# Layer 1's experts with 32 slots each, two experts on the tensor engine at once

## The chip, the core and the metric

The kernel is one program on one core of a Trainium2 chip. A core has a tensor engine (PE; its weight loads are listed apart, as PEld), a vector engine (DVE), a scalar engine (ACT), GpSimd (POOL), and SyncE (SP), which in this kernel issues every DMA. The metric is the device time of one run in microseconds (us), as the median of the runs; less is better.

## The reference, cut to what matters

The model has two layers (0 and 1). A layer mixes the tokens (attention, RWKV-7, mLSTM) and then sends them through a mixture of 32 SwiGLU experts. Layer 0 works on 512 tokens; layer 1, the last, on 256. The router picks one of four groups of eight experts for a token, and two experts of that group:

```python
def expert_block(args):
    xb, e = args                                  # rows of the tokens that chose expert e
    gate, up = jnp.split(xb @ w_gu[e], 2, axis=-1)     # w_gu[e]: 1024 x 1024
    return (jax.nn.silu(gate) * up) @ w_down[e]        # w_down[e]: 512 x 1024
...
out = jnp.zeros((N, D), f32).at[st].add(ys[dest] * sw[:, None])
```

All numbers are float32. The weights of one expert are 12 slices of 128 x 1024 (eight of `w_gu`, four of `w_down`), 0.524 MB each. On the reference's own inputs the router gives the 32 experts of layer 0 between 19 and 50 tokens each, and those of layer 1 between 6 and 24.

## The kernel before, in words

Each layer has a mixing phase and an expert phase (`moe_phase`). The order in which instructions stand on each engine is the order in which the program emits them; every engine works through its own list in order, and semaphores hold it where an operand or a buffer is not ready.

The expert phase goes through the experts one by one, with a fixed number of 64 slots for the tokens of each. For each expert `e` these stages are emitted, spread over the loop's steps so that neighbours mix:

- `stageA` (every second expert): picks the rows of two experts' tokens by products with a 0/1 matrix (`select`, `gather`) and transposes them (`turn`) into `xs`.
- `stageB(e, k)` for k from 0 to 7: products of `xs` (128 x 64) with slice k of the gate and up weights. The gate half of the columns goes to rows 0 to 63 of the PSUM bank, the up half to rows 64 to 127: two groups of 64 columns of the array. A float32 product shows as two records in the trace, so a slice is four records. After k = 7 ACT copies the bank to `rows`.
- `rows_of(e)`: one product with `rkT`, from which DVE makes the scatter matrix `selt`. There is one per expert.
- `swiglu`: four transposes on PE, silu on ACT, a product on DVE, giving `at`.
- `stageD(e, f)` for f from 0 to 3: products of `at` with the slices of `w_down`, again in two groups of 64 columns; then `parts`: for each half n of the columns ACT writes weighted rows of one half of the bank (`yy`) and DVE what rounding left, to the other half.
- `stageS`: four products that scatter `yy` to the tokens, in layer 1 added up over all experts in four PSUM banks (`acc`).

The weights come by the function `feeder`. It has a list of slices in the order of use (`seq`: for each expert four gate/up slices, the four down slices of the expert before, four more gate/up slices) and, in layer 1, buffers for 29 slices: one of four, ten of two, five of one. `pump` puts the next slices of the list into the next free buffer and emits a DMA for each run of slices that are neighbours in memory; `done(e, k)` counts a buffer's slices down where the program has emitted their last use, and calls `pump` again. On the chip the DMA waits on SP until PE has done that last use. DMAs take turns on eight landing semaphores, and an issue waits for the landing of the eighth before it.

Before the second expert the program emits `rest()`: what the routing still owes (ranks turned, slot weights `wsl`, and a flag `need` that tells whether any expert has more tokens than slots). After the last expert that flag is read, and only if it is set does a loop over blocks of 64 further slots run, with the weights loaded again for each block.

Ahead of layer 0's mixing, and partly within it, stands the conditioning: products of a small stationary tile with the slices `adaw`, in four groups of 32 columns.

Behind the experts of layer 1 lie the last sums on DVE, the final norm and the store of the output.

Of the kernel before, what the change touches and what calls it, by code (L numbers as in the profile page):

```python
# [20 lines left out]
SLOTS = 64  # L21
# [8 lines left out]
# columns of w_in by block: (first column, width); the gates' block carries repeats as filler  # L30
# [44 lines left out]
# columns of the per-layer parameter tile  # L75
# [8 lines left out]
# columns of the constants  # L84
CC = {}
_o = 0
for _n, _w in (("id", 128), ("perm", 128), ("cos", 256), ("sin", 256), ("mND", 256), ("mI", 128),
               ("bd", 64), ("neg", 256), ("blk", 128), ("tri", 128), ("ones", 128),
               ("rst64", 512), ("rst128", 512), ("hsel", 2), ("ie", 32), ("iot4", 4),
               ("s64", 128), ("sm", 64), ("pm", 1)):  # L90
    CC[_n] = (_o, _o + _w)
    _o += _w
# [3 lines left out]
# which stream's step comes next in the mixing of each layer  # L96
# [21 lines left out]
class Streams:  # L118
    """streams of instructions, merged step by step in the order of emission.

    A stream yields what its next step needs: None, a flag or a tuple of flags.
    """
# [13 lines left out]
    def step(self, it):  # L136
        """the stream's next step; True when it was the last"""
# [5 lines left out]
    def run(self, streams):  # L143
        """in the given order (a character per step, the first stream is "A"), or in turns"""
# [19 lines left out]
def program(tc, I, out, dbg=None, stop=None):  # L164
# [67 lines left out]
    # ---------------- dram scratch  # L232
# [30 lines left out]
    # ---------------- conditioning  # L263
# [26 lines left out]
    def mix_phase(l, last, TT0, hp, hr, rp, rt):  # L290
        X0 = 256 if last else 0           # first token of blocks that only feed outputs
        S0 = TT0 // 2                     # first segment with outputs
# [11 lines left out]
        def L(name, shape=(128, 512)):  # L304
            """outlasts the tiles of H"""
# [5 lines left out]
        def rsq(o, x, scale, eps, n):  # L311
            """o = (x * scale + eps) ** -0.5 on few columns"""
# [10 lines left out]
        # ================= conditioning: 1024 columns at a time, a quarter on each quarter of the rows  # L323
        def ada(la, pairs, first=None):
            """two groups at a time, on each quarter of the rows half a group"""
# [15 lines left out]
            for gi, g in enumerate(pairs):  # L341
# [15 lines left out]
                # columns of the shifts and scales, rows of the rest  # L357
# [12 lines left out]
        def consts():  # L370
            """the parameters and the other constants, behind what comes first"""
# [8 lines left out]
        # ================= norm, transpose  # L380
        hT = {}

        def norm():
# [39 lines left out]
            for k in range(KT):  # L423
# [4 lines left out]
                onact = k in (0, 2, 3, 5, 6)                # a bank is read by one engine  # L428
# [18 lines left out]
        # ================= input projection: weights loaded ahead, split one block ahead  # L447
# [56 lines left out]
        def by_tokens(name, o):  # L504
            """a block of the projection with the tokens on the rows"""
# [10 lines left out]
        # ================= differential attention  # L516
# [3 lines left out]
        def lam():  # L520
# [10 lines left out]
            stt(nlam, le[:, 1:2], -lam_init, le[:, 0:1], ADD, SUB)      # -(lam)  # L531
# [5 lines left out]
        def da_head(h):  # L537
# [3 lines left out]
            def rope(name, o, t0):  # L541
                """ctx columns copied, x columns turned"""
# [19 lines left out]
            # rounded parts and what is left on the two halves of the rows  # L562
# [69 lines left out]
        # ================= RWKV  # L632
# [60 lines left out]
        def rw_stack():  # L693
            """the operands of the small products, each below the other: rounded, what is left, rounded"""
# [24 lines left out]
        def rw_kk(b):  # L719
            """normalised keys, decays and rates of one pair of heads"""  # L720
# [45 lines left out]
        def rw_elem(d, b):  # L766
# [15 lines left out]
            pin = H("pin")                                  # half of the inverse decay  # L782
# [16 lines left out]
            km = H("km")                                    # twice the key  # L799
# [30 lines left out]
        def rw_scores(d, b):  # L830
# [3 lines left out]
            md_all = MDt[0]                                   # [row in its block, column, unit]  # L834
            ae, kp, bt = AB[d, b]
            LT[d, b] = H1("LT", [128, 4, 2, 32])              # the other 32-block of a chunk
            for j in range(4):
# [12 lines left out]
                nd = H1("nq", [128, 2, 2, 64])                # k or b, head  # L850
# [47 lines left out]
        def rw_chunks(d, b):  # L898
            """the inverses of the 64-blocks from those of their 32-blocks; turned, for products"""
# [8 lines left out]
            ks = [slice(64 * c + 32 * d, 64 * c + 32 * d + 32) for c in range(2)]       # sources  # L908
            os = [slice(64 * c + 32 - 32 * d, 64 * c + 64 - 32 * d) for c in range(2)]  # targets
# [19 lines left out]
        def rw_chain(d, b):  # L929
            """solves and the state's recursion for one direction and pair of heads"""  # L930
# [19 lines left out]
            for step in range(4):  # L950
# [18 lines left out]
                if full:  # L969
                    qr = H1("qr", [128, 2, 2, 64])            # [source in the chunk, k or b, head, target]  # L970
# [7 lines left out]
                # two chunks: G, B; yc  # L978
# [69 lines left out]
        def ln64(Y, eps, name, T2):  # L1048
            """layer norm over 64 columns of a [128, 512] tile in place; two token tiles"""
# [43 lines left out]
        # ================= mLSTM  # L1093
        ml = {"mk": {}, "mq": {}, "so": {}}

        def ml_post():
# [5 lines left out]
            for n in [x for x in order if x[0] == "m"]:  # L1102
# [17 lines left out]
                else:                                 # twice silu of the convolution  # L1120
# [582 lines left out]
    def moe_phase(l, last, TT0, rp, mp, rt):  # L1703
# [74 lines left out]
        def stageB(e, k):  # L1778
            if k == 0:
                GU[e] = PS()  # L1780
# [30 lines left out]
        def stageD(e, f):  # L1811
            if f == 0:
                PY[e] = PS()
# [267 lines left out]
```

## Time and profile before

| what | value |
|---|---|
| median of 3 runs | 1975.69 us (1973.17, 1975.69, 1977.97) |
| span of the profiled execution, first to last instruction | 1967.8 us |
| PE busy over the span | 1814.8 us (92%) |
| DVE, ACT, POOL busy | 1045.8, 614.2, 586.9 us |
| moved by DMA | 540.72 MB, mean 275 GB/s |
| expert phase of layer 1, first to last issue of its weights | 1417 to 1917 us |

The page of the profile gives the span of the profiled execution and no other time of it; the median of the runs is 7.9 us above that span. Busy times of PE come from modelled ends of matmuls, so that a busy PE says that products were in flight, and not that it was at its best. A DMA share of 1 means that the sixteen DMA engines of the core had packets in hand all the time.

### The profile page before, as it was taken

To read this page: it belongs to the slowest core of one execution; us is meant where nothing else is said; L and a number is where in the kernel's file an instruction comes from. 1 tells how busy PE (TensorE), PEld (TensorE's weight loads), DVE (VectorE), ACT (ScalarE), POOL (GpSimd) and SP (SyncE) were. 2 spreads that over 40 slices of the span, in tenths; PEclk is the share of its full clock that TensorE was granted. 3 is DMA by queue.
4 is the path that set the end of the run, shared out by engine and by line. 5 is a ranking of instruction groups with operands and counts; after the bars stand their busy time and mean duration, and the time that the engine had idled before them with its cause. 6 is when DMAs were issued, how large, how long until landed. Compare 5 with 4: busy or idle time off the path is not lost. (4 is left out here: it accounts for less than half of the span.)

```text
span 1967.8 us, 29955 instructions
## 1 busy us (share of the span) xinstructions
PE 1814.8 (92%) x11356; PEld 958.3 (49%) x11357; DVE 1045.8 (53%) x2156; ACT 614.2 (31%) x1308; POOL 586.9 (30%) x479
## 2 busy tenths in 40 slices
PE   6999999989699999999999598899869999999996
PEld 2666776656343333333333376767633333333332
DVE  3798656657545555455455689876752222221223
ACT  2453546641111111111111355447512112111121
POOL 1440222314135555655566453222310000000000
PEclk9999999988799999999999799989989999999998
DMA  8465646563979999999995333312589999999992
GB/s 337 138 219 183 201 142 220 209 216 125 368 294 353 377 343 364 362 369 366 359 368 203 109 101 119 119 49 88 190 319 394 405 412 415 412 414 415 413 414 87
DMA packets 171237, 540.72 MB, mean 275 GB/s; under 512 B 16464, under 2 KB 40272, under 8 KB 170960
## 3 DMA queue, kind: packets, MB, share of 16 engines
q1 hardware_dynamic: 171088, 538.75, 72.4%
q8 instruction: 92, 1.51, 0.3%
q14 instruction: 57, 0.47, 0.1%
HBM read 524.66 MB, written 13.96 MB: 274 GB/s over the span
## 5 line engine op out<-in xcount | busy, mean ns | idle before, releaser
L199 PE MATMUL ps<-wm,xs 128*64 128x512 f32 x2048 | 509.4, 609 | 0.0
L188 POOL TENSOR_TENSOR X<-X,tmp 128x512 f32<-128x512 f32 x252 | 321.9, 1307 | 271.0 <-DVE tmp L188 269.7
L199 PE MATMUL ps<-hT,spl 128*128 128x512 f32 (+2 forms) x1344 | 321.5, 393 | 8.4 <-ACT spl L185 3.0
L196 DVE SCALAR_TENSOR_TENSOR yy<-ps,wsl,yy 64x512 fp32r<-64x512 f32 x128 | 95.9, 750 | 373.3 <-ACT yy L185 373.3
L199 PEld LDWEIGHTS ps<-hT,spl 128*128 128x128 f32 (+1 forms) x1344 | 241.4, 197 | 69.2 <-issue 5.3
L199 PE MATMUL ps<-wm,at 128*64 128x512 f32 x1024 | 230.7, 592 | 0.9 <-DVE at L188 0.9
L199 PEld LDWEIGHTS ps<-wm,xs 128*64 128x64 f32 x2048 | 119.4, 136 | 201.9 <-issue 190.4
L185 ACT ACTIVATE yy<-ps,wsl 64x512 fp32r<-64x512 f32 x128 | 87.4, 683 | 375.2 <-PE ps L199 323.2
L188 DVE TENSOR_TENSOR tmp<-ps,g 128x512 f32<-128x512 f32 x256 | 164.5, 683 | 31.7 <-PE ps L199 24.3
L1938 POOL TENSOR_TENSOR fm<-fm,mhalf 128x1 f32<-128x1 f32 x2 | 1.1, 540 | 511.7 <-DVE fm L193 511.7
L199 PEld LDWEIGHTS ps<-wm,at 128*64 128x64 f32 x1024 | 73.4, 137 | 146.8 <-issue 144.2
L199 PE MATMUL ps<-h,sel 128*128 128x512 f32 x384 | 111.0, 427 | 10.4 <-DVE sel L188 10.4
L192 DVE TENSOR_SCALAR selt<-ps,cst 128x512 fp32r<-128x512 f32 (+1 forms) x64 | 39.5, 617 | 133.8 <-PE ps L199 133.8
L199 PEld LDWEIGHTS ps<-h,sel 128*128 128x128 f32 x384 | 70.7, 197 | 74.4 <-DVE sel L188 26.0
L185 ACT ACTIVATE rows<-ps 128x512 f32<-128x512 f32 x64 | 38.2, 597 | 183.7 <-PE ps L199 183.7
L185 ACT ACTIVATE xr<-ps 128x512 f32<-128x512 f32 x64 | 38.3, 598 | 180.2 <-PE ps L199 180.2
L199 PE MATMUL ps<-yy,selt 128*128 128x512 f32 x256 | 90.8, 437 | 1.9 <-DVE yy L196 1.9
L188 POOL TENSOR_TENSOR spl<-win,spl 128x1024 fp32r<-128x1024 f32 x20 | 49.8, 2491 | 100.5 <-ACT spl L185 100.5
L188 DVE TENSOR_TENSOR at<-sil,ps 128x256 f32<-128x256 f32 x64 | 26.9, 421 | 87.6 <-ACT sil L185 87.6
L199 PE MATMUL ps<-adaw,cs__104 128*32 128x512 f32 x384 | 60.4, 639 | 13.4 <-DMA adaw<-in_adaw_dram 13.2
L185 ACT ACTIVATE sil<-ps 128x256 f32<-128x256 f32 x64 | 24.6, 384 | 145.2 <-PE ps L230 145.0
L185 ACT ACTIVATE spl<-win 128x1024 fp32r<-128x1024 f32 (+1 forms) x56 | 58.6, 1051 | 26.1 <-DMA win<-in_win_dram 22.3
(471 smaller groups left out, 2622.0 us busy)
## 6 DMA issues: line engine op xcount, KB each, us to landing
wm<-in_gu_dram SPq DMA_DIRECT2D x151, 1024.0 KB
wm<-in_gu_dram SPq DMA_DIRECT2D x183, 512.0 KB
wm<-in_dn_dram SPq DMA_DIRECT2D x73, 1024.0 KB
wm<-in_dn_dram SPq DMA_DIRECT2D x100, 512.0 KB
adaw<-in_adaw_dram SPq DMA_DIRECT2D x96, 512.0 KB
win<-in_win_dram SPq DMA_DIRECT2D x54, 512.0 KB
wm<-in_gu_dram SPq DMA_DIRECT2D x5, 1536.0 KB
wraw<-in_wout_dram SPq DMA_DIRECT2D x24, 256.0 KB
```

Of the source, the lines that this page charges most:

```text
L185: return ACT.activation(o, i, f, **kw)
L188: return (eng or DVE).tensor_tensor(o, a, b, op=op)
L192: return (eng or DVE).tensor_scalar(o, a, s1, None, op0=op0)
L196: return DVE.scalar_tensor_tensor(o, a, s, b, op0=op0, op1=op1, **kw)
L199: return PE.matmul(o, l, r, start=start, stop=stop)
L1938: POOL.tensor_tensor(m_[:, 1:2], m_[:, 0:1], mhalf[:, 0:1], op=ALU.pow)
```

## The change

Layer 0 stays as it is: 64 slots, one expert at a time. In layer 1 an expert has 32 slots, and two experts form a unit: 16 units take the place of 32 experts in the loop.

- In `stageB` and `stageD` the two experts of a unit use the four groups of 32 columns of the array: expert x of the unit has rows 64x to 64x+31 for one half of the columns and rows 64x+32 to 64x+63 for the other (`share`). A step k or f takes a slice of each expert.
- `feeder` interleaves the two experts' slices, two and two: slices k and k+1 of the first, then of the second.
- `stageA` gathers for two units (four experts), `rows_of`, `swiglu`, `parts` and `stageS` work on a unit. `parts` has four pairs of ACT and DVE instructions of 32 rows for a unit, in place of two pairs of 64 rows for an expert.
- `rest()` writes `wsl` in two copies, and the flag is set where an expert has more than 32 tokens; the loop behind it still takes blocks of 64 (four of them in place of three).
- The constants have 129 more columns (`s32`, `pm32`).

```diff
-SLOTS = 64
+SLOTS = (64, 32)
+OVER = 64
...
     def feeder(l, last, pool):
-        seq = [(0, k) for k in range(8)]
-        for e in range(1, NE):
-            seq += [(e, k) for k in range(4)] + [(e - 1, 8 + k) for k in range(4)] + [(e, k) for k in range(4, 8)]
-        seq += [(NE - 1, 8 + k) for k in range(4)]
+        U = 64 // SLOTS[l]
+        NU = NE // U
+        def part_of(u, a, b):
+            return [(U * u + x, k + i) for k in range(a, b, 2) for x in range(U) for i in range(2)]
+        seq = part_of(0, 0, 8)
+        for u in range(1, NU):
+            seq += part_of(u, 0, 4) + part_of(u - 1, 8, 12) + part_of(u, 4, 8)
+        seq += part_of(NU - 1, 8, 12)
...
+        share = lambda x, i: slice((2 * x + i) * SL, (2 * x + i + 1) * SL)
+        def stageB(u, k):
             if k == 0:
-                GU[e] = PS()
-            gate_up(GU[e], XS[e // 2][:, :, e % 2 * 64:e % 2 * 64 + 64], WT[e, k], k)
-            done(e, k)
+                GU[u] = PS()
+            for x in range(U):
+                c = u % 2 * 64 + x * SL
+                for i in range(2):
+                    mm(GU[u][share(x, i), :], XS[u // 2][:, k, c:c + SL],
+                       WT[U * u + x, k][:, i * 512:(i + 1) * 512], k == 0, k == 7)
+            for x in range(U):
+                done(U * u + x, k)
...
-        def parts(ps, w):
+        def parts(ps, w, U=U):
             yy = TB("yy", (1024,), 2)
             ys = [yy[:, 0:512], yy[:, 512:1024]]
+            SL = 64 // U
             for n in range(2):
-                q, o = QS[n], QS[1 - n]
-                act(R(ys[n][q, :]), ps[q, :], AF.Copy, scale=w[q])
-                stt(R(ys[n][o, :]), ps[q, :], w[q], ys[n][q, :], MUL, SUB)
+                for x in range(U):
+                    q, o = (slice((2 * x + i) * SL, (2 * x + i + 1) * SL) for i in (n, 1 - n))
+                    act(R(ys[n][q, :]), ps[q, :], AF.Copy, scale=w[q])
+                    stt(R(ys[n][o, :]), ps[q, :], w[q], ys[n][q, :], MUL, SUB)
             return ys
...
+            for x in range(U):
+                for n in range(2):
+                    mm(PY[u][share(x, n), :], AT[u][:, f, x * SL:(x + 1) * SL],
+                       WT[U * u + x, 8 + f][:, n * 512:(n + 1) * 512], f == 0, f == 3)
...
-        for e in range(NE + 2):
-            g = (e + 1) // 2 if e % 2 and e + 1 < NE else None
+        for e in range(NU + 2):
+            g = (e + 1) // 2 if e % 2 and e + 1 < NU else None
...
-        nb = T // SLOTS - 1
+        nb = -(-(T - SL) // OVER)
```

PE's list in layer 1, before, from the product with `rkT` of the last expert but one to that of the last (`wm` are the weight slices, `xs` and `at` the rows they meet; a shape is that of the output, and xN counts equal products in a row):

```order
L199 MATMUL ps<-rkT,idr 128x256
L199 MATMUL acc<-yy,selt 128x512
L199 MATMUL ps<-wm,xs 64x512 x2
L230 MATMUL ps<-cst,rows 128x128 x4
L199 MATMUL acc<-yy,selt 128x512
L199 MATMUL ps<-wm,xs 64x512 x2
L199 MATMUL acc<-yy,selt 128x512
L199 MATMUL ps<-wm,xs 64x512 x2
L199 MATMUL ps<-wm,at 64x512 x8
L199 MATMUL acc<-yy,selt 128x512
L199 MATMUL ps<-wm,xs 64x512 x8
L199 MATMUL ps<-rkT,idr 128x256
```

The same place in the list of the change, from the last unit but one to the last:

```order
L200 MATMUL ps<-rkT,idr 64x256 x2
L200 MATMUL acc<-yy,selt 128x512
L200 MATMUL ps<-wm,xs 32x512 x4
L231 MATMUL ps<-cst,rows 128x128 x4
L200 MATMUL acc<-yy,selt 128x512
L200 MATMUL ps<-wm,xs 32x512 x4
L200 MATMUL acc<-yy,selt 128x512
L200 MATMUL ps<-wm,xs 32x512 x4
L200 MATMUL ps<-wm,at 32x512 x16
L200 MATMUL acc<-yy,selt 128x512
L200 MATMUL ps<-wm,xs 32x512 x16
L200 MATMUL ps<-rkT,idr 64x256 x2
```

The list of a unit is that of an expert before, stage by stage, with twice as many products of half the width wherever weight slices are used.

SP's list where layer 1's weights begin, before (`g` and `fg` are the rows of the last gates and of the final norm's gain; a shape with 2x or 4x is a DMA of two or four slices):

```order
L202 DMA wm<-in_gu_dram 128x4x1024
L202 DMA wm<-in_gu_dram 128x2x1024 x4
L202 DMA wm<-in_dn_dram 128x2x1024 x2
L202 DMA wm<-in_gu_dram 128x2x1024 x4
L202 DMA wm<-in_dn_dram 128x1024 x4
L202 DMA wm<-in_gu_dram 128x1024
L202 DMA g_14161<-modd_74 128x1024
L202 DMA fg<-in_fing_dram 128x1024
L202 DMA wm<-in_gu_dram 128x3x1024
```

And in the change:

```order
L203 DMA wm<-in_gu_dram 128x2x1024 x12
L203 DMA wm<-in_dn_dram 128x1024 x5
L203 DMA g_14162<-modd_74 128x1024
L203 DMA fg<-in_fing_dram 128x1024
L203 DMA wm<-in_dn_dram 128x1024
L203 DMA wm<-in_dn_dram 128x2x1024
L203 DMA wm<-in_gu_dram 128x1024 x16
```

Both fill the 29 buffered slices first; in the change the first 16 of them are the gate and up weights of the first two experts. The whole list of layer 1's weights has 251 DMAs before and 288 in the change, and it ends in the change with four DMAs of one slice each, the down slices 10 and 11 of the last two experts.

ACT's list at the last expert before (`yy` is what `parts` writes; DVE_49 and PE_49 are semaphores):

```order
L185 ACTIVATE rows<-ps 128x512 [waits PE_49,Activation_49]
L185 ACTIVATE sil<-ps 128x256 [waits PE_49,Activation_49]
L185 ACTIVATE yy<-ps,wsl 64x512 [waits PE_49]
L185 ACTIVATE yy<-ps,wsl 64x512 [waits DVE_49]
L1879 TENSOR_LOAD need [waits DMAHW2_49,DMAHW3_49,DMAHW1_49,DMAHW4_49,DMAHW0_49,DMAHW5_49,DVE_49,DMAHW6_49,PE_49,DMAHW7_49,Activation_49,Pool_49]
```

And at the last unit in the change:

```order
L186 ACTIVATE rows<-ps 128x512 [waits PE_49,Activation_49]
L186 ACTIVATE sil<-ps 128x256 [waits PE_49,Activation_49]
L186 ACTIVATE yy<-ps,wsl 32x512 [waits PE_49]
L186 ACTIVATE yy<-ps,wsl 32x512 [waits DVE_49] x3
L1916 TENSOR_LOAD need [waits DMAHW2_49,DMAHW3_49,DMAHW1_49,DMAHW4_49,DMAHW0_49,DMAHW5_49,DVE_49,DMAHW6_49,PE_49,DMAHW7_49,Activation_49,Pool_49]
```

Each ACT instruction of `parts` after the first waits for DVE's instruction of the pair before it: there is one such wait for an expert before, and there are three for a unit in the change. Up to the end of layer 1's mixing the lists of all engines are the same, but for the width of the DMA of the constants.

## Rows read from the trace of the kernel before

**Rows 1.** Windows: busy us (instructions) by engine, granted clock, DMA share, GB/s

```profile
16.00:31.00 15.00, 12.88 (x52) 1.73 (x48) 0.00 (x0) 0.00 (x0) 0.00 (x0) 1.00 1.03 420
1440.00:1470.00 30.00, 16.11 (x91) 11.25 (x91) 17.34 (x40) 5.43 (x8) 3.46 (x3) 0.72 1.03 413
...
1480.00:1490.00 10.00, 10.00 (x45) 3.69 (x45) 1.21 (x3) 3.54 (x5) 0.00 (x0) 0.97 0.84 314
1490.00:1500.00 10.00, 10.00 (x48) 3.56 (x48) 3.48 (x6) 1.66 (x3) 0.00 (x0) 1.00 1.03 406
1500.00:1900.00 400.00, 400.00 (x1727) 142.96 (x1723) 87.93 (x146) 78.06 (x133) 0.00 (x0) 1.00 1.02 413
1900.00:1925.00 25.00, 25.00 (x109) 9.28 (x109) 4.69 (x8) 4.38 (x8) 0.00 (x0) 1.00 1.02 412
...
1927.00:1928.00 1.00, 1.00 (x8) 0.34 (x6) 0.25 (x2) 0.68 (x1) 0.00 (x0) 1.00 0.25 102
1928.00:1929.00 1.00, 1.00 (x6) 0.29 (x4) 0.65 (x1) 0.00 (x0) 0.00 (x0) 1.00 0.00 0
...
1930.00:1945.00 15.00, 14.84 (x65) 5.17 (x61) 2.98 (x6) 3.09 (x6) 0.00 (x0) 1.00 0.01 1
```

**Rows 2.** DMA view, 1540 to 1600 us, 40 slices of 1.5 us

```profile
GB/s 407 415 423 418 410 306 355 385 393 418 418 421 423 401 404 410 410 415 404 412 412 407 410 407 410 415 410 423 418 418 418 437 396 421 421 426 415 418 410 415
```

**Rows 3.** Waits of weight loads, 1500:1900: total us, times, longest

```profile
PEld ps L199 <- DMA wm<-in_gu_dram: 2.3, 9, 0.4
PEld ps L199 <- DMA wm<-in_dn_dram: 1.0, 5, 0.3
```

**Rows 4.** Tile view, rkT in layer 1: ns min/median/max, first to last

```profile
L199 PE MATMUL ps<-rkT,idr x32: 377/380/577, 1480.2 to 1942.9; 32*128 32x256 f32 x32
```

**Rows 5.** Timeline of PE, one expert of layer 1: start, us, instruction

```profile
1615.33 0.38 PE L199 MATMUL ps<-rkT,idr 32*128 32x256 f32 x1
...
1616.06 1.08 PE L199 MATMUL ps<-wm,xs 128*64 128x512 f32 x4
...
1620.24 3.60 PE L199 MATMUL ps<-wm,at 128*64 128x512 f32 x16
...
1629.78 0.38 PE L199 MATMUL ps<-rkT,idr 32*128 32x256 f32 x1
```

**Rows 6.** Timeline of PE in layer 0, four groups of 32 columns

```profile
410.40 3.64 PE L199 MATMUL ps<-adaw,cs__104 128*32 128x512 f32 x16
...
418.97 1.92 PE L199 MATMUL ps<-adaw,cs__104 128*32 128x512 f32 x16
```

**Rows 7.** Timeline, PE and SP, where layer 1's experts start

```profile
1464.89 7.09 PE L199 MATMUL ps<-wm,xs 128*64 128x512 f32 x32
...
1468.59 3.76 SPq L202 DMA_DIRECT2D wm<-in_gu_dram  x4
...
1472.40 13.47 SPq L202 DMA_DIRECT2D wm<-in_dn_dram  x3
...
1476.74 1.50 PE L199 MATMUL ps<-wm,xs 128*64 128x512 f32 x4
```

**Rows 8.** Timeline where layer 1's experts end

```profile
1945.38 3.65 PE L199 MATMUL ps<-wm,at 128*64 128x512 f32 x16 [0.52 <-DVE at L188]
...
1949.08 0.68 ACT L185 ACTIVATE yy<-ps,wsl 64x512 fp32r<-64x512 f32 x1 [4.21 <-PE ps L199]
1949.80 0.74 DVE L196 SCALAR_TENSOR_TENSOR yy<-ps,wsl,yy 64x512 fp32r<-64x512 f32 x1 [4.47 <-ACT yy L185]
1950.57 0.68 ACT L185 ACTIVATE yy<-ps,wsl 64x512 fp32r<-64x512 f32 x1 [0.81 <-DVE yy L196]
...
1952.08 0.70 DVE L188 TENSOR_TENSOR acc<-acc,g 128x512 f32<-128x512 f32 x1
```

**Rows 9.** DMA issues on the page: count, KB each

```profile
adaw<-in_adaw_dram SPq DMA_DIRECT2D x96, 512.0 KB
```

More of the change, by code (lines that the diff above doesn't have):

```diff
@@ L1538, in routing @@
         T = 128 * NT
+        SL, U = SLOTS[l], 64 // SLOTS[l]
+        NU = NE // U
         lg = rt["lg"]
@@ L1633, in rest @@
                     sel = ssel[(s + j) % 2]
-                    ts(sel, C("s64"), rk[:, s, j:j + 1], None, EQ)
+                    ts(sel, C("s64" if SL == 64 else "s32"), rk[:, s, j:j + 1], None, EQ)
                     mm(pl, sel, tm[:, s, j], s + j == 0, s + j == NT)
-            rt["wsl"] = mp.tile([128, 32], F32, name="wsl")
-            DVE.tensor_copy(rt["wsl"], pl)
-            nb = T // SLOTS - 1
+            wsl = rt["wsl"] = mp.tile([128, NU], F32, name="wsl")
+            for x in range(U):
+                r = slice(2 * SL * x, 2 * SL * (x + 1))
+                DVE.tensor_copy(wsl[r], pl[r, x::U])
+            nb = -(-(T - SL) // OVER)
             pc = PS((128, 32))
@@ L1706, in moe_phase @@
         EQ = ALU.is_equal
+        SL, U = SLOTS[l], 64 // SLOTS[l]
+        NU, EG = NE // U, 2 * U
         def TB(name, sh, bufs):
@@ L1799, in down, with stageD, rows_of @@
                 mm(ps[QS[n], :], at[:, f, :], w[:, n * 512:(n + 1) * 512], f == 0, f == 3)
[L1801 removed]
+        def parts(ps, w, U=U):
             yy = TB("yy", (1024,), 2)
             ys = [yy[:, 0:512], yy[:, 512:1024]]
+            SL = 64 // U
             for n in range(2):
[L1806 to L1808 removed]
+                for x in range(U):
+                    q, o = (slice((2 * x + i) * SL, (2 * x + i + 1) * SL) for i in (n, 1 - n))
+                    act(R(ys[n][q, :]), ps[q, :], AF.Copy, scale=w[q])
+                    stt(R(ys[n][o, :]), ps[q, :], w[q], ys[n][q, :], MUL, SUB)
             return ys
[L1811 removed]
+        def stageD(u, f):
             if f == 0:
[L1813 to L1815 removed]
+                PY[u] = PS()
+            for x in range(U):
+                for n in range(2):
+                    mm(PY[u][share(x, n), :], AT[u][:, f, x * SL:(x + 1) * SL],
+                       WT[U * u + x, 8 + f][:, n * 512:(n + 1) * 512], f == 0, f == 3)
+            for x in range(U):
+                done(U * u + x, 8 + f)
             if f == 3:
[L1817 to L1819 removed]
+                Y[u] = parts(PY.pop(u), rt["wsl"][:, u:u + 1])
+        def rows_of(u):
             ps = PS((128, T))
[L1822 to L1824 removed]
+            n = 2 * SL
+            v = R if U == 1 else (lambda a: a)
+            for x in range(U):
+                e = U * u + x
+                mm(ps[n * x:n * x + n], v(rt["idr"][:, e:e + 1]).to_broadcast([32, n]), v(rt["rkT"]))
+            s = SELT[u] = TB("selt", (T,), 2)
+            ts(R(s), ps, C("pm" if SL == 64 else "pm32"), None, EQ)
         def add(j, n, ps, pool):
@@ L1914, in moe_phase @@
                         gate_up(ps, xs, wt, k)
-                    at = swiglu(evacuate(ps))
+                    at = swiglu(evacuate(ps), 1)
                     py = PS()
@@ L1920, in moe_phase @@
                         down(py, at, wt, f)
-                    ys = parts(py, w)
+                    ys = parts(py, w, 1)
                     ts(R(row), row, C("pm"), None, EQ)
```

52 lines of the change are left out of this document (25 added, 27 removed).

## The prediction

> **What bounds the kernel now.** The diff touches layer 1's expert phase alone, so I read that stretch first by windows [rows 1]. From 1500 to 1900 us two things are at their limit together: PE is busy in all 400 us, and the DMA engines have a share of 1.02 at 413 GB/s. The reader should see that this rate does not hang on PE: from 1440 to 1470, while the 29 buffers are being filled and PE is busy for 16.1 of 30 us, it is 413 as well. So 413 GB/s is what the transfers give. An expert is 12 slices of 0.524 MB, 6.29 MB, or 15.2 us at that rate.
>
> Which of the two sets the end? The waits of the weight loads say that PE hardly ever waits for a slice: 3.3 us of 400 [rows 3]. The 32 products with `rkT`, one per expert, run from 1480.2 to 1942.9, 14.9 us per expert [rows 4]. PE therefore needs slightly less than the transfers, but it starts late: its first products with weights stand at 1464.89 [rows 7], when nearly all 29 buffers are full, and at 0.3 us per expert it never makes up that delay. At the end this shows openly: the last traffic of the weights falls in 1927 to 1928, and from 1930 to 1945 PE is busy for 14.8 of 15 us with nothing moving [rows 1]. The last products with weights begin at 1945.38 and ACT takes their result at 1949.08 [rows 8]: about 21 us behind the transfers. That backlog is what a faster PE can win; the transfers themselves it cannot shorten, except where they starved for buffers.
>
> **The change part by part.**
>
> *Products with weights.* In an expert [rows 5] the first slice has 4 records in 1.08 us, and four slices 16 records in 3.60, so a further slice costs 0.84 us; 12 slices are 10.1 of the 14.9 us. In the change a round of eight records serves two slices in four groups of 32 columns. Layer 0's conditioning uses just this form: 16 records of four groups take 1.92 us at the full clock [rows 6], against 3.60 for 16 records of two groups. Twice the records at half the price: a unit's weight products cost PE what an expert's cost. The other stages stand once per unit as they stood once per expert, so I take 14.9 us of PE for a unit, 7.5 per expert, against 30.5 us of transfers. PE makes up its delay in the first units and then waits for slices; the stage is bound by transfers to its end.
>
> *Transfers.* The same 201.3 MB. What can be gained is where they starved. After the first expert PE freed buffers slowly, since it stood in `rest()` until 1476.74; SP spent 13.5 us over three issues from 1472.40 on [rows 7], and the rate fell to 314 in 1480 to 1490 and 406 in the next 10 us [rows 1], a loss of 10 x 99/413 + 10 x 7/413 = 2.6 us. A second dip, four slices of 1.5 us at 306, 355, 385 and 393 [rows 2], lost 1.5 x 213/413 = 0.8 us. In the change unit 0 uses 16 slices before `rest()` where expert 0 used 8, in about the same 7.09 us [rows 7]; that frees 4.2 MB more, 10 us of transfers, which covers the gap. I take the whole 3.4 us as won; the other bound is nothing. The end of the traffic moves from 1928.0 to 1924.6.
>
> *From the last bytes to ACT.* The landing must reach PE. No row shows this lag alone; below it is nothing, above it I take 1 us, what the first slice costs in records [rows 5]. I choose 0.5, in the middle, as nothing leans to an end. The list ends with single-slice DMAs, so one round of eight records remains: 4 records of two groups, 1.08 us, is its upper bound and my value, as the first half of the round may already be through. ACT starts at 1924.6 + 0.5 + 1.1 = 1926.2, before at 1949.08: 22.9 us earlier. The swiglu of the last unit ends well ahead: behind its slices eight down slices still come, 10 us.
>
> *The tail of `parts`.* ACT and DVE take turns: from one ACT instruction to the next it is 1.49 us, from 1949.08 to 1950.57, and two such pairs fill the time until DVE begins the last sums at 1952.08 [rows 8]. Four pairs, each waiting for the one before, cost 2 x 1.49 = 3.0 us more if 32 rows take as long as 64: the instructions have the same 512 columns. No row shows 32 rows; the other bound is half of the price, 0 us more. I take 3.0. Within the stage this chain is hidden: 6 us of 30.5. Queued behind it on DVE are the last sums, which wait anyway. What follows is unchanged.
>
> *At no cost:* the second copy of `wsl`, the fourth test for the flag, 129 columns of constants (0.07 MB, 0.2 us before layer 0 has its data). The waits of `rest()` are covered by buffered slices; uncovered they would cost below 1 us.
>
> *Sum:* 22.9 - 3.0 = 19.9 us earlier. The span goes from 1967.8 to 1947.9. The runs' median lies 7.9 us above the profiled span, and I carry that over: 1975.7 - 19.9 = **1955.8 us**.
>
> **The limit of the transfers, weighed.** The queue was full between 1440 and 1470 and still gave 413 GB/s; conditioning, in 16 to 31 us, got 420 [rows 1]. So a deeper queue may give between 413 and 420: 1.7% of some 485 us, up to 8 us less, 1947.8; I stay at 413, the nearer row. The Trainium skill's page "DMA: Bandwidth & Descriptors", section "Where 436 GB/s comes from", puts the ceiling at 435 GB/s, set by the ports of the SBUF; by it an estimate of the sum would be 24 us lower still. The trace does not reach it anywhere in this stage, with the queue full or not.
>
> **The rivals.**
>
> *The clock falls.* PE will now wait for slices. Where it was busy for 16.1 of 30 us, the granted clock was 0.72 on average [rows 1], between the two levels of 1.2 and 2.4 GHz; and four groups at the lower level took 3.64 in place of 1.92 us [rows 6]. Then a unit costs 2 x 14.9 = 29.8 us of PE, just under the 30.5 of the transfers: PE keeps up, but with little slack. The end pays some 6 us: a last round at half speed, and up to three of the last four rounds still queued (1.7 us each). That gives 1962. Against it: in conditioning the transfers set the pace too, PE was busy 12.9 of 15 us, and the clock was 1.00 [rows 1]. The Trainium skill's page "TensorE: Matmul & The Clock Gate", section "HAM oscillation — how this bites in real kernels", describes such a kernel, whose short bursts of products between waits for DMA each start at the lower clock; the window of conditioning disagrees, that of 1440 to 1470 agrees.
>
> *Packing does not come.* Were the two experts' products to run one pair after the other, a unit would cost 29.8 us, PE would stay as far behind as now, and only the 3.0 us of `parts` would remain: 1978.7, within 0.2%. Against it stand the records of [rows 6].
>
> *Smaller transfers.* 288 DMAs in place of 251, eight at most in flight. If the rate fell by 4%, to 396, it would eat the gain: 1975. Against it: conditioning's transfers are of 512 KB, one slice, all 96 of them [rows 9], and moved at 420.
>
> *Slower: the loop for overflow.* If any expert of layer 1 had over 32 tokens, its block would load 12 slices (15.2 us) and use them (14.9 us) with little overlap, behind the phase: 30 us or more, 1986 at least. It decides from the 33rd token on; the largest count on the reference's inputs is 24, so it should not happen.
>
> **How the numbers follow.** Transfers to the end, as summed: 0.80. Lower clock: 0.08. Rate above 415: 0.04. Packing missing: 0.02. Slower transfers, eating most of the gain: 0.04. Overflow or another loss: 0.02. A measurement of this kernel tells about 0.2%, 4 us, from no change. Faster 0.92, same 0.05, slower 0.03. For the range I take the bounds: 1947.8 (420 GB/s) and, upwards, no starvation regained (+3.4), 1 us of lag (+0.5) or the lower clock (+6): 1963. With the medians' own spread of 2 us: 1947 to 1964.
>
> **What the profile of the change would show.** Right: in the last hundreds of us of the phase PE's weight loads wait for DMA of `wm`, some 15 us in 30; the rate stays at 413 with no dip from 1480 to 1500; products with `rkT` stand 30.5 us apart; the last weight products begin within 2 us of the last bytes; four ACT instructions `yy` stand 1.5 us apart at the end. Wrong: PE busy throughout with units 30 us apart (packing), a clock well below 1 in that stretch, a rate under 400, or 32-row `yy` instructions that cost half. The prediction falls if the transfers can run faster than 420 once PE no longer holds them, or if they slow down beside four groups of columns.

## The result, and the profile after

The changed kernel takes 1953.27 us (median of 4 runs, 1949.34 to 1953.61), the kernel before beside it 1974.43 us (4 runs, 1972.66 to 1977.97). The ratio is 0.9892, with a 95% interval of 0.9863 to 0.992: faster by 21.2 us. The profiled execution has a span of 1951.7 us, 16.1 less than before.

Profiled executions begin layer 1's experts some us apart: PE's first product with `wm` stands between 1459.6 and 1476.9 in the eleven that have two experts on PE at once, and between 1461.6 and 1468.7 in the three that have one. The change touches what lies ahead only by a wider DMA of constants. So the phase is compared from that product to the end of the span: before 1967.8 - 1464.89 = 502.9 us [rows 7], after 1951.7 - 1470.72 = 481.0 us, 21.9 less. The unchanged kernel of the change was run beside the kernel before three times, with 21.2, 18.4 (`after_again`) and 18.3 us (`after_third`) between the medians; that a part of the 21.9 us is lost again ahead of the phase is not excluded.

The windows of the changed kernel, with the columns of [rows 1] (busy us and instructions of PE, PEld, DVE, ACT and POOL, granted clock, DMA share, GB/s):

```profile
16.00:31.00 15.00, 12.75 (x52) 1.72 (x48) 0.00 (x0) 0.00 (x0) 0.00 (x0) 1.00 1.02 413
...
1470.00:1480.00 10.00, 8.38 (x70) 2.38 (x68) 2.76 (x12) 1.16 (x5) 0.00 (x0) 0.94 1.02 417
1480.00:1490.00 10.00, 8.77 (x36) 4.17 (x36) 3.59 (x18) 1.88 (x2) 0.00 (x0) 0.58 1.03 417
1490.00:1500.00 10.00, 10.00 (x76) 3.63 (x76) 1.16 (x2) 1.85 (x4) 0.00 (x0) 0.91 1.03 408
1500.00:1900.00 400.00, 302.22 (x1562) 74.38 (x1554) 65.93 (x103) 58.00 (x95) 0.00 (x0) 0.95 1.03 415
1900.00:1925.00 25.00, 18.79 (x95) 4.36 (x97) 3.90 (x6) 3.69 (x6) 0.00 (x0) 0.86 1.03 416
1925.00:1930.00 5.00, 3.33 (x26) 0.68 (x20) 0.00 (x0) 0.00 (x0) 0.00 (x0) 1.00 0.47 190
1930.00:1945.00 15.00, 3.33 (x9) 1.20 (x5) 8.54 (x14) 4.90 (x8) 0.54 (x1) 0.68 0.01 2
```

From 1500 to 1900 PE's busy time fell from 400 us to 302, and the transfers moved at 415 GB/s in place of 413. The dip of 1480 to 1490 (314 GB/s before) is gone. At the end, PE's work and the traffic now stop together: the 15 us of PE's work with nothing moving are no longer there.

The waits of the same 400 us (in all, times, longest), as in [rows 3], and SP's own from its list:

```profile
PEld ps L200 <- DMA wm<-in_gu_dram: 113.6, 75, 3.7
PEld ps L200 <- DMA wm<-in_dn_dram: 77.2, 47, 3.7
...
SPq L203 <- DMA wm<-in_gu_dram: 154.9, 135, 2.5
SPq L203 <- DMA wm<-in_dn_dram: 72.6, 67, 2.2
SPq L203 <- PE ps L200: 29.2, 28, 4.7
```

The roles have changed sides. The weight loads waited 3.3 us for slices before and wait 190.8 now. SP, whose DMAs stood behind PE, now stands behind landings; before, its list had:

```profile
SPq L202 <- PE ps L199: 271.4, 147, 7.9
```

The tile view has the products with `rkT` (four records a unit):

```profile
L200 PE MATMUL ps<-rkT,idr x64: 374/424/684, 1487.6 to 1921.4; 32*64 32x256 f32 x64
```

The 15 intervals from the first to the last have a mean of 28.9 us, below the 30.5 of the transfers, since the first units run on filled buffers. Of the 15, the ten from the fifth product to the fifteenth take (1894.95 - 1590.46)/10 = 30.4 us each. PE's timeline of that stretch shows the rhythm, bursts of products and after each a wait for a slice (in brackets: idle before, and what ended it):

```profile
1590.46 0.65 PE L200 MATMUL ps<-rkT,idr 32*64 32x256 f32 x4
...
1604.76 1.91 PE L200 MATMUL ps<-wm,at 128*32 128x512 f32 x12 [1.51 <-DMA wm<-in_dn_dram]
...
1607.31 1.05 PE L200 MATMUL ps<-wm,xs 128*32 128x512 f32 x4 [0.21 <-DMA wm<-in_gu_dram]
1609.88 1.05 PE L200 MATMUL ps<-wm,xs 128*32 128x512 f32 x4 [1.52 <-DMA wm<-in_gu_dram]
...
1894.95 0.65 PE L200 MATMUL ps<-rkT,idr 32*64 32x256 f32 x4
```

The timeline where the phase starts, and where it ends, answers to [rows 7] and [rows 8]:

```profile
1470.72 7.33 PE L200 MATMUL ps<-wm,xs 128*32 128x512 f32 x64
...
1928.44 1.07 PE L200 MATMUL ps<-wm,at 128*32 128x512 f32 x8 [1.47 <-SPq L1917]
1929.70 1.05 PE L200 MATMUL ps<-wm,at 128*32 128x512 f32 x4 [0.19 <-SPq L1917]
...
1930.80 0.68 ACT L186 ACTIVATE yy<-ps,wsl 32x512 fp32r<-32x512 f32 x1 [7.71 <-PE ps L200]
1931.51 0.74 DVE L197 SCALAR_TENSOR_TENSOR yy<-ps,wsl,yy 32x512 fp32r<-32x512 f32 x1 [7.97 <-ACT yy L186]
1932.28 0.68 ACT L186 ACTIVATE yy<-ps,wsl 32x512 fp32r<-32x512 f32 x1 [0.81 <-DVE yy L197]
...
1935.98 0.76 DVE L197 SCALAR_TENSOR_TENSOR yy<-ps,wsl,yy 32x512 fp32r<-32x512 f32 x1 [0.75 <-ACT yy L186]
1936.77 0.70 DVE L189 TENSOR_TENSOR acc<-acc,g 128x512 f32<-128x512 f32 x1
```

The last weight products wait for the last slices: the profile names SP's wait at the flag behind the phase (L1917), where the landings are waited for, and the traffic runs out at 1929.0. Then comes the longer chain of `parts`: 5.97 us from ACT's first `yy` to DVE's first sum, 3.00 before.

### The profile page after: what moved, and what is told of

It reads as the page before. It is cut to its first block, busy times and chain, and to the rows that moved or that the text cites. A ratio compares the mean times of both kernels' runs of the same rounds, so it can differ in the third digit from the quotient of the medians.

```text
span 1951.7 us, 29308 instructions
## 1 busy us (share of the span) xinstructions
PE 1687.5 (86%) x11132; PEld 876.3 (45%) x11133; DVE 1016.0 (52%) x2102; ACT 588.7 (30%) x1260; POOL 587.1 (30%) x479
## 5 line engine op out<-in xcount | busy, mean ns | idle before, releaser
L200 PE MATMUL ps<-wm,xs 128*64 128x512 f32 (+1 forms) x2048 | 443.4, 626 | 62.2 <-DMA wm<-in_gu_dram 59.7
L197 DVE SCALAR_TENSOR_TENSOR yy<-ps,wsl,yy 64x512 fp32r<-64x512 f32 (+1 forms) x128 | 95.8, 749 | 382.5 <-ACT yy L186 382.5
L200 PE MATMUL ps<-wm,at 128*64 128x512 f32 (+1 forms) x1024 | 212.4, 617 | 43.8 <-DMA wm<-in_dn_dram 40.5
L200 PEld LDWEIGHTS ps<-wm,xs 128*64 128x64 f32 (+1 forms) x2048 | 90.0, 124 | 275.1 <-issue 136.5
L186 ACT ACTIVATE yy<-ps,wsl 64x512 fp32r<-64x512 f32 (+1 forms) x128 | 87.1, 680 | 403.4 <-PE ps L200 338.4
L200 PEld LDWEIGHTS ps<-wm,at 128*64 128x64 f32 (+1 forms) x1024 | 54.4, 124 | 190.0 <-issue 97.9
L200 PE MATMUL ps<-h,sel 128*128 128x512 f32 x320 | 92.2, 430 | 10.4 <-DVE sel L189 10.4
L200 PEld LDWEIGHTS ps<-h,sel 128*128 128x128 f32 x320 | 60.1, 200 | 61.2 <-DVE sel L189 26.4
L186 ACT ACTIVATE xr<-ps 128x512 f32<-128x512 f32 x48 | 28.7, 597 | 176.2 <-PE ps L200 162.6
L200 PEld LDWEIGHTS ps<-yy,selt 128*128 128x128 f32 x256 | 39.6, 189 | 49.9 <-issue 43.0
L186 ACT ACTIVATE sil<-ps 128x256 f32<-128x256 f32 x48 | 18.4, 383 | 137.9 <-PE ps L231 137.9
```

Of the source, the lines that this page charges most:

```text
L186: return ACT.activation(o, i, f, **kw)
L197: return DVE.scalar_tensor_tensor(o, a, s, b, op0=op0, op1=op1, **kw)
L200: return PE.matmul(o, l, r, start=start, stop=stop)
```

## The experiments

Each kernel was timed against the kernel before on the same chip, one chip for each of three groups: `after_again`, `tail`, `feed_by_expert`, `no_packing` (before: 1969.52 us); `before_cut`, `double`, `triple`, `after_once` (before: 1969.15 us); the last four (before: 1972.62 us). "Phase" is, as above, from PE's first product with `wm` to the end of the span of the profiled execution. The ratios are not quotients of the medians shown, by which `after_again` and `after_third` both stand at 0.9907 and `tail_again` at 0.986.

| label | median us (range) | ratio to before [95%] | phase us |
|---|---|---|---|
| after_again | 1951.11 (1944.64 to 1959.21) | 0.9911 [0.988, 0.9942] | 481.7 |
| tail | 1949.87 (1939.67 to 1952.75) | 0.99 [0.9876, 0.9924] | 478.0 |
| feed_by_expert | 1952.5 (1948.99 to 1964.82) | 0.9921 [0.989, 0.9951] | 481.5 |
| no_packing | 1951.2 (1940.55 to 1957.86) | 0.9898 [0.9866, 0.9929] | 482.7 |
| before_cut | 1956.4 (1950.34 to 1964.28) | 0.9929 [0.9898, 0.996] | 485.9 |
| double | 1955.78 (1953.0 to 1960.77) | 0.9924 [0.9897, 0.9952] | 487.4 |
| triple | 2069.04 (2065.6 to 2073.46) | 1.05 [1.0452, 1.0547] | 597.8 |
| after_once | 1769.55 (1767.7 to 1774.6) | 0.8983 [0.8943, 0.9024] | 300.3 |
| before_once | 1969.9 (1964.61 to 1979.74) | 0.9986 [0.9961, 1.0012] | 505.8 |
| no_packing_once | 1792.93 (1784.7 to 1796.97) | 0.9061 [0.9018, 0.9105] | 324.6 |
| after_third | 1954.29 (1946.34 to 1960.2) | 0.9876 [0.9841, 0.9911] | 481.5 |
| tail_again | 1945.08 (1940.61 to 1951.51) | 0.9844 [0.9808, 0.9879] | 477.6 |

### What set the pace before: no reloads

```diff
-                kind, cap = free.pop(0)
-                if kind == "r":
+                kind, cap, *old = free.pop(0)
+                if old:
+                    w = old[0]
+                elif kind == "r":
...
-                left[sid] = [len(part), (kind, cap)]
+                left[sid] = [len(part), (kind, cap, w) if last else (kind, cap)]
...
-                    dma(w[:, i:i + n, :], wsrc(*part[i], n))
+                    if not old:
+                        dma(w[:, i:i + n, :], wsrc(*part[i], n))
```

**before_once** (this edit on the kernel before). 

> The kernel before with the weights of layer 1 loaded only until the 29 buffers are full once; later experts use what the buffers hold, so values differ and the order of PE's work stays. Theory (before, PE and not the transfers set the pace of layer 1's experts, 14.9 us per expert): the time stays within 4 us of the kernel before, at most 3 us shorter for the starved loads, and the products with rkT stand 14.8 to 14.9 us apart. Rival (the transfers set the pace before as well, 15.2 us per expert, and PE only looks busy because its ends are modelled): the phase shortens by clearly more than 10 us.

Some 186 MB of transfers are gone, and the time is the same: 0.9986 with 1 inside the interval, and a phase that is not shorter. The products with `rkT` stand (1942.9 - 1478.4)/31 = 15.0 us apart, 0.1 us above what was expected. The first window below is of this kernel:

```profile
1500.00:1700.00 200.00, 200.00 (x864) 71.72 (x862) 42.56 (x71) 39.31 (x67) 0.00 (x0) 1.00 0.00 1
```

PE fills every one of the 200 us with nothing moving. Before the change the transfers were not the limit, though their share read 1.02 all along: the theory holds.

**after_once** (the same edit on the changed kernel). 

> The changed kernel with layer 1's weights loaded only until each buffer has been filled once (29 slices of 384); later slices are computed with what lies there, so values differ. PE is then held by nothing. Theory: a unit costs PE 14.9 us, 16 units 239 us in place of 480: about 1738. Rival (packing gives less than a factor of two): with products at the old price 1738 + 168 = 1906.

The same edit is worth 180 us here. A unit takes (1738.5 - 1482.1)/15 = 17.1 us, so the transfers stretch it by 13.4 us to 30.5. Not all of that shows as idle time: PE was idle for 97.8 of 400 us in the change, 7.5 us in a unit. But a slice that comes alone is used in four records that take 1.05 us, where eight take 1.07 (the timelines above). The 17.1 us are not the 14.9 that the prediction took, and the expected time of 1738 is missed by 32 us. In its window and waits of 1500 to 1700:

```profile
1500.00:1700.00 200.00, 182.35 (x1303) 58.91 (x1306) 52.32 (x84) 48.06 (x79) 0.00 (x0) 0.95 0.00 1
```

```profile
PEld ps L200 <- ACT rows L186: 27.3, 11, 2.6
...
PE ps L200 <- DVE sel L189: 10.5, 6, 1.8
...
PE ps L200 <- DVE xs L1773: 7.1, 5, 1.4
```

PE is idle for 17.65 of 200 us, 1.5 us in a unit. The timeline shows for whom:

```profile
1576.46 3.62 PE L200 MATMUL ps<-wm,at 128*32 128x512 f32 x32
...
1580.15 0.68 ACT L186 ACTIVATE yy<-ps,wsl 32x512 fp32r<-32x512 f32 x1 [5.67 <-PE ps L200]
1580.43 4.50 PE L200 MATMUL ps<-wm,xs 128*32 128x512 f32 x40
...
1585.32 0.60 ACT L186 ACTIVATE rows<-ps 128x512 f32<-128x512 f32 x1
1585.33 0.76 DVE L197 SCALAR_TENSOR_TENSOR yy<-ps,wsl,yy 32x512 fp32r<-32x512 f32 x1 [0.75 <-ACT yy L186]
1586.12 0.42 DVE L189 TENSOR_TENSOR sel<-cst,rkE 128x256 fp32r<-128x256 f32 x1
1586.69 1.16 PE L200 MATMUL ps<-h,sel 128*128 128x512 f32 x4 [1.76 <-DVE sel L189]
```

The four pairs of `parts` hold ACT and DVE for 6 us. PE meanwhile has finished the gate and up products, and ACT's `rows` and DVE's `sel` come behind the chain. That the remaining 0.7 us come from the clock of 0.95 is only argued.

### How much PE work the transfers hide: double and triple

```diff
-            for x in range(U):
+            for rep in range(U):
+                for x in range(U):
...
-                       ..., k == 0, k == 7)
+                       ..., k == 0 and rep == 0, k == 7 and rep == U - 1)
```

The down products have the same edit; in `triple` the count is 3.

**double.** 

> The changed kernel with every product with weights of layer 1 done twice into the same sums (values differ). PE's work of a unit rises from 14.9 to about 25.2 us, below the 30.5 us of transfers. Theory: the changed kernel's time plus 1 us for the last round, 1953 to 1957. Rival (PE is still near the limit): up to 16 x 10 = 160 us more.

Twice the weight products leave the median about where it was: 0.9924 against 0.9911 for the change itself, intervals overlapping.

```profile
1500.00:1900.00 400.00, 378.55 (x2919) 115.17 (x2915) 66.66 (x104) 58.96 (x96) 0.00 (x0) 1.00 1.03 414
```

PE is busy for 378.55 of the 400 us, at a clock of 1.00, and its loads wait 56.8 us for slices in place of 190.8. In the profiled execution the phase is 5.7 us longer than in `after_again`, where the doubled rounds do lie open: the rate falls to 314 GB/s from 1490 to 1500 again, and PE ends the last down products at 1930.2 without a gap, when the traffic has been over since 1927.5. Whether the runs are longer too, their spread does not tell.

**triple.** 

> The same products three times. PE's work of a unit is about 35.5 us, above the 30.5 us of transfers. Theory: PE sets the end again, 16 x 35.5 = 568 us in place of the 480 that 32 experts cost before, 2060 to 2070. Rival (PE has more slack than thought, for instance a unit of 10 us): below 2000.

Now PE is the bound: (2032.3 - 1500.6)/15 = 35.4 us per unit, its loads wait 1.5 us of 400 for slices, and the rate falls to 349 GB/s:

```profile
1500.00:1900.00 400.00, 400.00 (x3437) 125.78 (x3439) 54.19 (x85) 49.54 (x80) 0.00 (x0) 1.00 0.91 349
```

A repetition of the weight products costs (35.4 - 17.1)/2 = 9.2 us, so that `double` asks about 26 us of PE for a unit: the point from which PE decides lies between 26 and 35.4.

### Which part of the change is needed

**no_packing**: the feeder's list goes by expert, and PE does four slices of one expert and then four of the other, so that two groups of 32 columns take turns at a time.

```diff
-            return [(U * u + x, k + i) for k in range(a, b, 2) for x in range(U) for i in range(2)]
+            return [(U * u + x, k) for x in range(U) for k in range(a, b)]
...
-                for i in range(2):
-                    mm(GU[u][share(x, i), :], XS[u // 2][:, k, c:c + SL],
+                for kk in range(k - 3, k + 1) if U == 2 and k % 4 == 3 else () if U == 2 else (k,):
+                    for i in range(2):
+                        mm(GU[u][share(x, i), :], XS[u // 2][:, kk, c:c + SL],
...
+                    done(U * u + x, kk)
```

The down products have the same edit, all four slices of one expert first.

> Edit: on top of the list by expert, PE does the first expert's products of four slices, then the second's, so that only two groups of 32 columns are in use at a time. Theory: a unit then costs PE about 20.6 + 4.8 = 25.4 us, still below the 30.5 us of its transfers, so within 2 us of the changed kernel: in time, sharing gather, transposes, swiglu and scatter is enough. Rival (the gain comes from four groups at once): back to the kernel before, 1974, or near 1978 with the longer parts.

It is as fast as the change (0.9898 against 0.9911). Its loads still wait for slices, 71.5 us of the 200 from 1500, against 94.8 in `after_again`.

**no_packing_once** (the same with no reloads). 

> The change with the two experts of a unit worked on one after the other (two groups of 32 columns at a time) and the weights loaded only until the buffers are full once; values differ. This shows what packing is worth to PE where no transfer hides it. Theory (four groups halve the price of the weight products, 10.1 us per unit): with weights loaded once a unit took 17.1 us with packing, so without it 17.1 + 10.1 = 27.2 us, less up to 2 us of waits that it covers: 25 to 27.2 us, a time of about 1769.6 + 16 x 9 = 1905 to 1931. As this is under the 30.5 us of the transfers, it also says why the change without packing was as fast. Rival (packing brings nothing on PE): 17.1 us as with packing, 1770. Second rival (PE needs 29.8 us as two experts before): 1970.

Missed by both rivals and by the theory: a unit takes (1765.9 - 1488.1)/15 = 18.5 us, only 1.4 us more than with packing. The timeline of this kernel says why:

```profile
1603.63 4.09 PE L200 MATMUL ps<-wm,xs 128*32 128x512 f32 x26
1607.13 0.62 PE L200 MATMUL ps<-wm,at 128*32 128x512 f32 x2
1607.55 0.60 PE L200 MATMUL ps<-wm,xs 128*32 128x512 f32 x2
1607.59 0.60 PE L200 MATMUL ps<-wm,at 128*32 128x512 f32 x2
1607.98 0.60 PE L200 MATMUL ps<-wm,xs 128*32 128x512 f32 x2
...
1613.76 5.38 PE L200 MATMUL ps<-wm,xs 128*32 128x512 f32 x32
```

In PE's list all 32 records of `wm,xs` stand ahead of the first `wm,at`, but those of `wm,at` for the first expert, whose two groups are idle, start while the last six of `wm,xs` have not. So PE does not start these records strictly in the order of its list, as the section on the kernel has it of every engine, and the edit did not take packing away: a record costs 5.38/32 = 0.168 us, between the 0.113 of four groups (3.62 us for 32 in `after_once`) and the 0.225 of two groups of 64 [rows 5]. What PE would need with no overlap at all was not measured, and `no_packing` shows only that the exact order is not needed.

**feed_by_expert**: the list alone by expert (the first line of the diff above), PE's order as in the change. 

> Edit: the feeder's list is not interleaved any more; of each stretch come the first expert's slices, then the second's. Theory: with 29 buffered slices the order within a unit does not matter to a stage that is bound by transfers; one round is left after the last slice as before; within 2 us of the changed kernel. Rival (interleaving is what keeps buffers turning): buffers are held longer, transfers starve, 5 to 20 us more.

No difference that can be measured (phase 481.5 against 481.7). The longest wait for a slice is 8.6 us from 1500 to 1700, where an expert's slices arrive after the other's, and it costs nothing, though the granted clock is lower than the 0.95 of the change: the transfers never stop.

```profile
1500.00:1900.00 400.00, 293.79 (x1550) 80.94 (x1544) 65.79 (x102) 58.56 (x95) 0.00 (x0) 0.83 1.03 415
```

### The backlog alone: less PE work in the kernel before

**before_cut**, in layer 1:

```diff
-            down(PY[e], AT[e], WT[e, 8 + f], f)
+            if not last:
+                down(PY[e], AT[e], WT[e, 8 + f], f)
+            elif f < 2:
+                for n in range(2):
+                    mm(PY[e][QS[n], :], AT[e][:, f, :], WT[e, 8 + f][:, n * 512:(n + 1) * 512], f == 0, f == 1)
```

> The kernel before, with half of the down products of layer 1 left out (slices 10 and 11 of each expert are loaded and released, not used), so its numbers differ. PE saves 1.7 us per expert, 13.2 in place of 14.9. Theory (the backlog): only the delay of PE behind the transfers can be won, 21 to 23 us, and perhaps part of the 3 us of starvation: 1949 to 1954. Rival (the stage follows PE's work): 32 x 1.7 = 55 us, 1920.

The 1.7 us that this takes from an expert (two slices at 0.84 us) bring PE from just under the 15.2 us of the transfers to well under it, 13.2, and the phase falls by 17.0 us with nothing else of the change: PE catches up and then waits, in 1500 to 1900:

```profile
PEld ps L199 <- DMA wm<-in_gu_dram: 28.7, 27, 3.5
PE ps L199 <- DMA wm<-in_gu_dram: 14.4, 15, 2.6
```

ACT takes the last product 1935.81 - 1468.65 = 467.2 us after PE's first, against 484.2 before and 460.1 in the change. The 7 us between the last two have two causes. Some 4 are the transfers': they starve here as they did before (the first window below; 408 GB/s in the change), and the traffic runs out 1930.7 - 1468.65 = 462 us after PE's first product, 458 in the change. The other 3 are lost behind the traffic, from which ACT's start is 5.1 us away, 1.8 in the change, as a window and the timeline of PE show:

```profile
1490.00:1500.00 10.00, 10.00 (x46) 3.23 (x42) 3.37 (x5) 2.53 (x4) 0.00 (x0) 1.00 0.88 305
...
1929.00:1930.00 1.00, 1.00 (x4) 0.24 (x2) 0.00 (x0) 0.00 (x0) 0.00 (x0) 0.50 0.45 184
```

```profile
1926.04 5.39 PE L199 MATMUL ps<-wm,xs 128*64 128x512 f32 x12 [2.62 <-SPq L1884]
1931.35 0.53 PE L199 MATMUL ps<-rkT,idr 32*128 32x256 f32 x1
...
1933.82 1.94 PE L199 MATMUL ps<-wm,at 128*64 128x512 f32 x8 [0.52 <-DVE at L188]
```

After its wait PE runs the last 12 gate and up records at a granted clock of 0.50, the level of 1.2 GHz: 0.45 us each, 2.7 us more than at 0.225, a part of it while traffic still runs. Then the swiglu, 2.5 us from 1931.35 to 1933.82, lies open, since with one expert at a time it does not end ahead of the last down slices.

### The open end: the chain of parts

**after_again**, the change unchanged, for this comparison. 

> The changed kernel as it is, to stand beside the next three on the same chip. Theory (the backlog): PE used to run some 21 us behind the transfers at the end, the change wins that and pays 3 us in parts, so 1953 to 1956 us here too. Rival (the transfers run faster beside a less busy PE): the same time, so this run does not tell them apart.

**tail**: the two halves of the columns in two PSUM banks, so that ACT's next instruction need not wait for DVE's, and half of the last additions on GpSimd.

```diff
-                PY[u] = PS()
+                PY[u] = [PS() for _ in range(U)]
...
+                pairs = [(0, 0), (1, 0), (0, 1), (1, 1)]
+                at_(*pairs[0], True)
+                for i, p in enumerate(pairs):
+                    if i < 3:
+                        at_(*pairs[i + 1], True)
+                    at_(*p, False)
...
+                    if n == 0:
+                        o = TB("xr", (512,), 2)
+                        tt(o, acc[j, n], g2[1][:, c], MUL)
+                        tt(rt["X"][j + TT0][:, c], rt["X"][j + TT0][:, c], o, ADD, POOL)
+                        continue
```

(`at_` with True is ACT's instruction of a pair, with False DVE's.) 

> Edit: in layer 1 the down products of the two halves n go to two PSUM banks, parts is ordered so that ACT works on one bank while DVE reads the other, and half of the last additions run on POOL. Theory (the chain of parts and the sums behind the last slice lie bare at the end, all else is covered by transfers): ACT to the first of the last sums 3.8 us in place of 6.0, the sums 4.1 in place of 5.4, together 3.5 us less than the changed kernel, 1950. Rival (two more banks in use stall PE or the chain is limited elsewhere): no gain, or some us more.

**after_third** and **tail_again**, the same two once more, on another chip. 

> The change unchanged, beside the next kernel: 1951 to 1953, as before.

 

> The change with the last parts on two PSUM banks, ACT and DVE overlapping, and half of the last sums on GpSimd, again beside the change in the same call. Theory (the chain of parts and the sums behind it lie open at the end): 2 to 4 us less than the change, 1947 to 1950. Rival (the end is hidden behind something else): the same as the change.

The timeline of `tail_again` at its end:

```profile
1925.73 2.94 ACT L186 ACTIVATE yy<-ps,wsl 32x512 fp32r<-32x512 f32 x4 [5.16 <-PE ps L200]
1926.44 3.08 DVE L197 SCALAR_TENSOR_TENSOR yy<-ps,wsl,yy 32x512 fp32r<-32x512 f32 x4 [5.42 <-ACT yy L186]
...
1929.62 0.69 DVE L189 TENSOR_TENSOR xr<-acc,g 128x512 f32<-128x512 f32 x1
```

ACT's four instructions run without a gap, and from the first to DVE's first sum it is 3.89 us in place of 5.97. The phase is 3.7 us shorter in the first pair of profiled executions and 3.9 us in the second. The medians differ by 1.2 us in the first pair and 9.2 us in the second, and the intervals of the ratios overlap; that it is faster is shown in the profile, by how much in the runs is not. It is the fastest version measured that does the whole work.

## Why the prediction was right

It named 1955.8 us, 19.9 less than before; the runs gave 1953.27, 21.2 less than the kernel before beside them. The 7.9 us that it carried over from span to median were no property of the kernel: here the median lies 1.6 us above the span, and the span of 1947.9 that it summed was 3.8 short of 1951.7. By its steps, from PE's first product with `wm`:

| step | forecast us | measured us |
|---|---|---|
| end of the traffic | -3.4 | 458.3 - 463.1 = -4.8 |
| from there to ACT taking the last product | 1.6 - 21.1 = -19.5 | 1.8 - 21.1 = -19.3 |
| the two together | -22.9 | 460.1 - 484.2 = -24.1 |
| chain of `parts` at the end | +3.0 | 5.97 - 3.00 = +2.97 |
| after it | 0 | 14.9 - 15.7 = -0.8 |
| phase | -19.9 | -21.9 |

- **PE's backlog was most of the gain,** 19.3 of the 24.1 us. That PE, at 14.9 us per expert, set the pace although the DMA share read 1.02 is shown from both sides: leaving out the reloads changes nothing before (`before_once`), and a little less PE work alone wins 17.0 us (`before_cut`).
- **The transfers are the bound now.** With the weight products done twice, about 26 us of PE for a unit, the phase grows by 5.7 us in place of the 16 x 9.2 = 147 that PE has more to do; at 35.4 us per unit PE decides. The rate was put at 413 GB/s and is 415 (1500 to 1900).
- **The starved loads came back.** The rate is 417 and 408 from 1480 to 1500, where it was 314 and 406, and PE's first run of 64 records took 7.33 us, forecast about 7.09. The traffic runs out some 5 us earlier, against a forecast of 3.4. It seems to take both the 16 slices ahead of `rest()` and their lower price: `before_cut`, with 8 slices, keeps the dip and ends its traffic at 462 us, and so does `double`, with 16 slices at twice the work (463.7).
- **The chain of parts** cost what the prediction chose, between bounds of nothing and 3.0, without a row that showed it: instructions of 32 rows take 0.68 and 0.75 us, as 64 rows do.
- **The mis-sized step** is "I take 14.9 us of PE for a unit". It is 17.1 us with the transfers away, since the chain of `parts`, "hidden: 6 us of 30.5", delays ACT and DVE for PE. The forecast did not suffer, since the slack of 13.4 us covers the error.
- **The rivals.** The clock did fall at times (0.58 in 1480 to 1490, 0.86 in 1900 to 1925), but its mean is 0.95 over 1500 to 1900 and nothing was behind at the end: the last products waited for slices. That the price is real where it strikes shows `before_cut`, whose last gate and up records fell into such a stretch and took 2.7 us longer; that it need not reach the time shows `feed_by_expert`, at a mean of 0.83. The Trainium skill's page "TensorE: Matmul & The Clock Gate", section "HAM oscillation — how this bites in real kernels", describes bursts that each start at the lower clock, in a kernel whose waits for DMA are longer than its bursts. The 400 us of the change, with PE busy for 302 of them and loads that waited up to 3.7 us, do not show that: 0.95 is mostly the upper of the two levels. Smaller transfers did not slow down (415 with 288 DMAs). Faster ones did not appear: 420 GB/s, the upper case, is itself no fixed level, as conditioning's window gives 413 in the execution after. The 435 GB/s of the Trainium skill's page "DMA: Bandwidth & Descriptors", section "Where 436 GB/s comes from", was reached in no window of 10 us or more that is shown. The prediction's "does not reach it anywhere in this stage" is too strong: one slice of 1.5 us in [rows 2] has 437, and the next 396. Packing was not missing: 3.62 us for 32 records (`after_once`). The rival's condition, two experts' products one pair after the other, did not even come about by reordering PE's list (`no_packing_once`), so a kernel with no packing at all was not measured. The loop for overflow did not run: behind the chain of `parts` come 14.9 us, in place of 15.7 before.

## What to carry to other kernels

Where two resources both read as full, look at the last microseconds of the phase: the one that still works when the other has stopped sets the end, and the backlog between the two is the most that a change to it can win, but for what the other lost by waiting for it (here 19.3 us and 4.8). Removing one of them altogether in an experiment (here the reloads) settles it, and tells at the same time how much slack the other edits may use up. A stage split into narrower pieces costs its chain once more at the open end, where it can be overlapped again.

## What the runs showed of the hardware

- PE started records of idle column groups ahead of earlier ones in its list: six records of `wm,xs` started after the first `wm,at` behind them (timeline of `no_packing_once`), and in the same kernel 32 records of nominally two groups took 5.38 us, not the 7.2 that 0.225 us each would give.
- ACT and DVE need as long for 32 rows of a PSUM bank as for 64: 0.68 and 0.75 us, at 512 columns.
- Where an expert's slices came one after the other, with waits up to 8.6 us, the granted clock was 0.83 over 400 us; interleaved, with waits up to 3.7 us, it was 0.95 (`feed_by_expert` and the change).
- A DMA share of 1.02 at 413 GB/s did not say that the transfers were the bound: with the reloads gone the time was the same.
